# Issuing the seven Strassen products of an MLP chunk between the up products of the next chunk

## The chip, the cores and the metric

The kernel runs on one core of a Trainium2 chip. A core has five engines with instruction queues of their own: TensorE (PE; its weight loads appear as PEld), VectorE (DVE), ScalarE (ACT), GpSimd (POOL) and SyncE (SP), which here issues the DMAs. The metric is device time in microseconds, lower is better. A profile is of one execution.

## The reference

A two-layer encoder on 512 tokens of width 1024, in float32. What matters here is the MLP of a layer and what follows it:

```python
h = rmsnorm(x, g_ffn[i])
u = dwconv(h @ w_up[i], w_ffn_conv[i])       # 1024 -> 2 * 2816, then a width-3 convolution over tokens
a, val = u[..., :D_FF], u[..., D_FF:]
x = x + (jax.nn.silu(a) * val) @ w_down[i]   # 2816 -> 1024
h = rmsnorm(x, g_ple[i])
pg = jax.nn.sigmoid(h @ w_ple_gate[i])
x = x + pg * (p[i] @ w_ple[i])
```

## The kernel before

**Precision.** Every float32 matmul is three: both operands are split into a high part in float32r and a remainder (`wh`, `wl` of a weight; `hh`, `hl`, `ah`, `al`, `gh`, `gl` of activations), and `mm3` (lines 89 to 91) issues high by high, low by high, high by low. The split is a cast on ScalarE and a subtraction on VectorE (`weight` for loaded weights, lines 84 and 85; `split`, lines 94 and 95). The pool `wp` has five buffers each for `wh` and `wl`, used by all weights, and three for the raw loads.

**Up products.** The 2816 hidden columns are 22 tiles of 128. For tile `j`, `gated` computes two up products (gate and value), each 24 matmuls of 512 columns into a PSUM tile `ps_mm` or `ps_sc` (two buffers each). `taps` applies the convolution to a product (`fa`: one operation on ScalarE, line 619, two on VectorE, 620 and 621), SiLU goes over the gate, and their product is written to half of a tile `gv` (line 645).

**Down products.** A pair of tiles makes one `gv`. Two pairs (four tiles, eight up products) make a chunk whose down product is done by Strassen's scheme in the Winograd form. `combos` makes four sums of the activation blocks (`ss`) on POOL and splits all seven operands (`ah`, `al`). `seven` loads four blocks of `w_down` (`b11` to `b22`, one pool with `t3`, five buffers), makes four combinations of them on POOL (lines 553, 554, 556, 558), splits seven weights, and issues seven products of 12 matmuls each into PSUM accumulators `r1`, `r2`, `r3` (two tiles each, tags `tp`, three buffers, and `av`, one). After a product, `residual` adds its accumulator to `xs` on VectorE (line 599). Three of the products (P4, P6, P7) go on accumulating in `r1` after it has been read, and P5 in `r3`.

**Chunks.** 22 tiles are five chunks of four and one pair left over. In the kernel before, the leftover pair comes first, as an ordinary product (`proj` with two row blocks), and the five chunks follow. In the last chunk, `norm` of rows 0 and 1 is issued after the fifth product, of rows 2 and 3 after the seventh.

**Order.** The code is recorded by a framework that orders each engine's instructions by a list scheduler with a model of time; buffers of a pool are given out in that order. Inside `tc.manual_schedule` for TensorE, TensorE's instructions keep the order of the code; the other queues are still ordered by the scheduler. Before, the MLP has no such region.

Of the kernel before, what the change touches and what calls it, by code (L numbers as in the profile page):

```python
# [11 lines left out]
F32 = mybir.dt.float32  # L12
F32R = mybir.dt.float32r
# [22 lines left out]
FF = 2816  # L36
NJ = FF // P
EPS = 1e-6
CHUNKS = ((0, 2), (2, 6), (6, 10), (10, 14), (14, 18), (18, 22))
HS = S // 2  # L40
MAGIC = 12582912.0
LAG1 = 2
# [17 lines left out]
def encoder_kernel(ctx, tc, x_in, pT, pos, inv, w_a1, w_z, w_g, w_uq, w_ukv, w_au, w_cu, w_o,  # L60
# [15 lines left out]
    def psum(tag="mm"):  # L76
        return ps.tile([P, S], F32, tag=tag, name="ps_" + tag, bufs={"mm": 2, "av": 1, "sc": 2, "tp": 3}[tag])
# [15 lines left out]
    def split(hi, lo, src):  # L93
        nc.scalar.copy(hi, src)  # L94
        nc.vector.tensor_sub(lo, src, hi.bitcast(F32))  # L95
# [93 lines left out]
    def layer(l, first):  # L189
# [348 lines left out]
        def wsplit(raw):  # L538
            h = wp.tile([P, 1024], F32R, tag="wh", name="wh")
            lo = wp.tile([P, 1024], F32R, tag="wl", name="wl")  # L540
            split(h, lo, raw)
            return h, lo

        def seven(pool, ops, blocks, add, done, tags):
            b11, b12, b21, b22 = (pool.tile([P, 1024], F32, tag="rawd", name=n, bufs=5)
                                  for n in ("b11", "b12", "b21", "b22"))
            for i, b in ((2, b21), (0, b11), (1, b12), (3, b22)):
                nc.sync.dma_start(b, blocks[i])
            t3 = pool.tile([P, 1024], F32, tag="rawd", name="t3", bufs=5)
# [3 lines left out]
            g.tensor_tensor(t3, b22, b12, ALU.subtract)
            g.tensor_tensor(b12, b12, b11, ALU.subtract)
            wt1 = wsplit(b12)
            g.tensor_tensor(b11, b11, t3, ALU.add)
            wt2 = wsplit(b11)
            g.tensor_tensor(b21, b21, b11, ALU.subtract)

            def product(o, a, w, first):  # L560
                for tt in range(2):
                    tk = slice(tt * P, (tt + 1) * P)
                    for i, (h, lo) in enumerate(ops):
                        c = slice(i * 512, i * 512 + 512)
                        mm3(o[tt], (h[:, a, tk], lo[:, a, tk]), (w[0][:, c], w[1][:, c]),
                            first and i == 0, i == len(ops) - 1, not first)

            def out(o, rows, n):
                for tt in range(2):
                    add(2 * rows + tt, n, o[tt])  # L570

            r2 = [psum(tags[2]), psum(tags[3])]
            product(r2, 1, w21, True)
            out(r2, 0, 0)
            r1 = [psum(tags[0]), psum(tags[1])]
            product(r1, 0, w11, True)
            out(r1, 0, 0)
            r3 = [psum(tags[2]), psum(tags[3])]
            product(r3, 3, wt1, True)
            out(r3, 1, 1)  # L580
            product(r1, 4, wt2, False)
            out(r1, 0, 1)
            w22 = wsplit(b22)
            product(r3, 6, w22, False)
            out(r3, 0, 1)
            done(0)
            done(1)
            wt3 = wsplit(t3)
            product(r1, 5, wt3, False)
            out(r1, 1, 1)  # L590
            wt4 = wsplit(b21)
            product(r1, 2, wt4, False)
            out(r1, 1, 0)
            done(2)
            done(3)

        def residual(t, n, o):
            c = slice(n * 512, n * 512 + 512)
# [30 lines left out]
            for i in range(NE):  # L629
                ws(eo[i][:, c], ew[i], hT, KD, P, 0, c)  # L630
        g3 = load_gain(l, 2, ff)
        def gated(j, v):
            av = []
            for i in (2 * j, 2 * j + 1):
                if i < NE:
                    o = eo[i]
                else:
                    w = weight(w_up[l, i])
                    o = psum("sc" if i % 2 else "mm")
                    ws(o, w, hT, KD, P, 0)  # L640
# [4 lines left out]
            nc.vector.tensor_tensor(v[:, j % 2, :], av[0], av[1], ALU.mult)

        for c, (j0, j1) in enumerate(CHUNKS):
            ops = []
            for j in range(j0, j1, 2):
                v = ff.tile([P, 2, S], F32, tag="gv", name="gv", bufs=2)  # L650
                gated(j, v)
                gated(j + 1, v)
                if c:
                    ops.append(combos(ff, v))
                else:
                    gh, gl = (ff.tile([P, 2, S], F32R, tag="gt", name=n, bufs=8) for n in ("gh", "gl"))
                    split(gh, gl, v)
            last = j1 == NJ
            if c:
                seven(ff, ops, w_down[l, 4 * c - 2:4 * c + 2], residual,  # L660
                      (lambda t: norm(t, g3, ff)) if last else (lambda t: None),
                      ("mm", "mm", "sc", "sc") if last else ("tp", "tp", "tp", "av"))
            else:
                KTOT = 2
                proj((lambda k, q: gh[:, k, q], lambda k, q: gl[:, k, q]), range(2), w_down[l], residual, ("tp",))
# [8 lines left out]
        KTOT = 2  # L674
# [33 lines left out]
def _layout(i):  # L708
    f = {n: np.asarray(a) for n, a in i.items()}
    w_in = f["w_in"]  # L710
    o_cb, o_cc, o_cx, o_g = A1, A1 + CW, A1 + 2 * CW, A1 + 3 * CW

    def mtiles(w):
        l, k, n = w.shape
        return w.reshape(l, k // P, P, n // P, P).transpose(0, 3, 2, 1, 4)

    def interleave(*ws):
        return np.stack([mtiles(w) for w in ws], 2)

    def halves(w):  # L720
        l, k, n = w.shape
        return w.reshape(l, k // 256, 2, P, 2, 512).transpose(0, 4, 1, 3, 2, 5).reshape(l, k // 128, P, 1024)

    z = interleave(w_in[:, :, o_cc:o_cx], w_in[:, :, o_cx:o_g], w_in[:, :, o_cb:o_cc])
    g = interleave(w_in[:, :, o_g:o_g + D], w_in[:, :, o_g + D:])
    uq = f["w_uq"].reshape(L, QL, H, DQK)
    uq = np.concatenate([uq[..., :DN].reshape(L, QL, H * DN), uq[..., DN:].reshape(L, QL, H * DR)], -1)
    ukv = f["w_ukv"].reshape(L, KVL, H, 2, 64).transpose(0, 1, 3, 2, 4).reshape(L, KVL, 1024)

    def up2(w):  # L730
        l, k, n = w.shape
# [35 lines left out]
    return {n: np.ascontiguousarray(a) for n, a in res.items()}
# [18 lines left out]
```

## Time and profile before

| | |
|---|---|
| Median of three runs | 1600.34 us (1596.21, 1600.34, 1600.38) |
| Profiled execution | 1597.0 us, its span 1595.2 us |
| TensorE busy | 1547.1 us, 97% of the span |
| VectorE busy | 1040.9 us, 65% |
| ScalarE busy | 726.7 us, 46% |
| GpSimd busy | 286.9 us, 18% |
| Mean granted TensorE clock | 0.991 |

A line such as `L599` is a line of the kernel before. The matmuls of line 89 to 91 carry the names of their output tile and operands, by which the products are told apart: `ps_mm` or `ps_sc` from `hh` and `wh` is an up product, `ps_tp` or `ps_av` from `ah` a product of `seven`. Busy time of TensorE is that of overlapping matmuls; their starts tell the rate.

### The profile page before, as it was taken

To read this page: it belongs to the slowest core of one execution; us is meant where nothing else is said; L and a number is where in the kernel's file an instruction comes from. 1 tells how busy PE (TensorE), PEld (TensorE's weight loads), DVE (VectorE), ACT (ScalarE), POOL (GpSimd) and SP (SyncE) were. 2 spreads that over 40 slices of the span, in tenths; PEclk is the share of its full clock that TensorE was granted. 3 is DMA by queue.
4 is the path that set the end of the run, shared out by engine and by line. 5 is a ranking of instruction groups with operands and counts; after the bars stand their busy time and mean duration, and the time that the engine had idled before them with its cause. 6 is when DMAs were issued, how large, how long until landed. Compare 5 with 4: busy or idle time off the path is not lost.

```text
span 1595.2 us, 18618 instructions
## 1 busy us (share of the span) xinstructions
PE 1547.1 (97%) x7168; PEld 1263.9 (79%) x7168; DVE 1040.9 (65%) x1384; ACT 726.7 (46%) x1136; POOL 286.9 (18%) x273
## 2 busy tenths in 40 slices
PE   7999999999999989999999999999999989998998
PEld 6888888888877778787888888888887878787776
DVE  7787543346776776778477774433566776767673
ACT  5578723234333333335374886322344333333452
POOL 2700000001223132321045000000012142222300
PEclk9999999999999999999999999999999999999999
DMA  6211222315231322213242112222342322323031
GB/s 205 89 53 40 64 94 94 106 53 187 70 116 66 119 65 94 94 65 99 63 132 80 40 40 80 93 94 78 113 149 70 119 66 92 102 83 106 27 99 60
DMA packets 41433, 142.08 MB, mean 89 GB/s; under 512 B 5761, under 2 KB 6273, under 8 KB 41345
## 3 DMA queue, kind: packets, MB, share of 16 engines
q1 hardware_dynamic: 41344, 140.90, 26.8%
q8 instruction: 56, 0.92, 0.2%
q14 instruction: 33, 0.26, 0.1%
HBM read 138.78 MB, written 2.10 MB: 88 GB/s over the span
## 4 chain that ended last, share of the span: by engine, by line
PE 88%; DVE 5%; POOL 3%; ACT 2%; issue 1%; DMA 0%; DVEq 0%; POOLq 0%; ACTq 0%
PE ps_mm L90 14%; PE ps_mm L89 14%; PE ps_mm L91 14%; PE ps_sc L89 10%; PE ps_sc L90 10%; PE ps_sc L91 10%; PE ps_tp L89 3%; PE ps_tp L90 2%; PE ps_tp L91 2%; PE ps_tp L429 2%; PE ps_av L89 1%; PE ps_av L90 1%; PE ps_av L91 1%; PE ps_tp L126 1%; POOL rs L100 1%; PE ps_av L441 1%
## 5 line engine op out<-in xcount | busy, mean ns | idle before, releaser
L84 ACT CAST wh<-raw 128x1024 fp32r<-128x1024 f32 (+1 forms) x210 | 219.1, 1046 | 415.8 <-PE ps_mm L90 125.0
L85 DVE TENSOR_TENSOR wl<-raw,wh 128x1024 fp32r<-128x1024 f32 (+1 forms) x210 | 273.6, 1304 | 198.0 <-ACT wh L84 191.5
L89 PE MATMUL ps_mm<-hh,wh 128*128 128x512 f32 (+1 forms) x832 | 326.4, 392 | 0.4 <-DVE ycv L356 0.4
L90 PE MATMUL ps_mm<-hl,wh 128*128 128x512 f32 (+1 forms) x832 | 322.7, 388 | 0.0
L91 PE MATMUL ps_mm<-hh,wl 128*128 128x512 f32 (+1 forms) x832 | 322.4, 387 | 0.0
L91 PEld LDWEIGHTS ps_mm<-hh,wl 128*128 128x128 f32 x832 | 156.6, 188 | 34.8
L89 PEld LDWEIGHTS ps_mm<-hh,wh 128*128 128x128 f32 x832 | 156.7, 188 | 33.0 <-DVE ycv L356 0.9
L90 PEld LDWEIGHTS ps_mm<-hl,wh 128*128 128x128 f32 x832 | 156.9, 189 | 32.4 <-DVE hl L95 0.4
L90 PE MATMUL ps_sc<-hl,wh 128*128 128x512 f32 (+1 forms) x368 | 142.1, 386 | 0.0
L91 PE MATMUL ps_sc<-hh,wl 128*128 128x512 f32 (+1 forms) x368 | 142.1, 386 | 0.0
L89 PE MATMUL ps_sc<-hh,wh 128*128 128x512 f32 (+1 forms) x368 | 142.0, 386 | 0.0
L99 POOL TENSOR_SCALAR ms<-ms 128x1 f32<-128x1 f32 (+2 forms) x40 | 14.1, 353 | 694.1 <-ACT junk L118 669.0
L95 DVE TENSOR_TENSOR wl<-b,wh 128x1024 fp32r<-128x1024 f32 x60 | 82.5, 1375 | 74.9 <-ACT wh L94 74.9
L89 PE MATMUL ps_tp<-wh,ah 128*128 128x512 f32 x176 | 73.4, 417 | 26.3 <-ACT ah L94 17.6
L599 DVE TENSOR_TENSOR xs<-xs,ps_tp 128x512 f32<-128x512 f32 x104 | 69.9, 681 | 21.3 <-PE ps_tp L91 20.9
L94 ACT CAST wh<-b 128x1024 fp32r<-128x1024 f32 x60 | 62.8, 1047 | 44.1 <-PE ps_sc L90 22.1
L90 PEld LDWEIGHTS ps_sc<-hl,wh 128*128 128x128 f32 x368 | 69.3, 188 | 15.4
L89 PEld LDWEIGHTS ps_sc<-hh,wh 128*128 128x128 f32 x368 | 69.3, 188 | 15.3
L91 PEld LDWEIGHTS ps_sc<-hh,wl 128*128 128x128 f32 x368 | 69.3, 188 | 15.3
L90 PE MATMUL ps_tp<-wl,ah 128*128 128x512 f32 x176 | 72.3, 411 | 0.0
L643 ACT ACTIVATE fa<-fa 128x512 f32<-128x512 f32 x44 | 27.8, 631 | 94.7 <-DVE fa L621 94.7
L91 PE MATMUL ps_tp<-wh,al 128*128 128x512 f32 x176 | 70.1, 406 | 0.0
(271 smaller groups left out, 3081.3 us busy)
## 6 DMA issues: line engine op xcount, KB each, us to landing
raw<-in_w_up_dram SPq DMA_DIRECT2D x88, 512.0 KB, 3.4
b<-in_w_down_dram SPq DMA_DIRECT2D x40, 512.0 KB, 3.4
raw<-in_w_g_dram SPq DMA_DIRECT2D x32, 512.0 KB, 3.5
raw<-in_w_z_dram SPq DMA_DIRECT2D x24, 512.0 KB, 3.5
raw<-in_w_o_dram SPq DMA_DIRECT2D x16, 512.0 KB, 3.4
raw<-in_w_pg_dram SPq DMA_DIRECT2D x16, 512.0 KB, 3.5
raw<-in_w_au_dram SPq DMA_DIRECT2D x8, 512.0 KB, 3.4
raw<-in_w_cu_dram SPq DMA_DIRECT2D x8, 512.0 KB, 3.5
```

What stands on the lines that cost most here:

```text
L84: nc.scalar.copy(h, raw)
L85: nc.vector.tensor_sub(lo, raw, h.bitcast(F32))
L89: nc.tensor.matmul(o, st[0], mv[0], start=start, stop=False, skip_group_check=more)
L90: nc.tensor.matmul(o, st[0], mv[1], start=False, stop=False, skip_group_check=more)
L91: nc.tensor.matmul(o, st[1], mv[0], start=False, stop=stop, skip_group_check=more)
L94: nc.scalar.copy(hi, src)
L95: nc.vector.tensor_sub(lo, src, hi.bitcast(F32))
L100: nc.gpsimd.tensor_tensor(r, ms, negh[:, :n], ALU.pow)
L126: nc.tensor.transpose(tp[:, j * P:(j + 1) * P], ht[:, j * P:(j + 1) * P], ident)
L429: nc.tensor.transpose(tp[:, k * P:(k + 1) * P], pe[:, k * P:(k + 1) * P], ident)
L599: nc.vector.tensor_tensor(xs[:, t, c], xs[:, t, c], o, ALU.add)
L643: nc.scalar.activation(a, a, AF.Silu)
```

## The change

`seven` becomes a generator with a `yield` after its loads and first two weight splits and after each product but the last. A list `work` holds it, and `step` runs it on by one product. `gated` calls `step` after each up product, so that a chunk's products stand one by one behind the up products of the next chunk; the weight splits and POOL combinations inside `seven` are moved to one or two products before their use. The MLP stands in a manual region for TensorE. The five chunks come first, the leftover pair last, with its four up products taking one, two, two and no steps behind them, so that the last two products stand behind the fourth; then `proj` of the leftover rows, whose second half of columns calls `norm`. The rows of `w_down` are laid out in the new order on the host. Line numbers below `seven` shift: 599 is now 602, 619 to 621 are 622 to 624, 645 is 656, 556 and 558 are 572 and 578.

```diff
-CHUNKS = ((0, 2), (2, 6), (6, 10), (10, 14), (14, 18), (18, 22))
+NQ = NJ // 4
...
             w21 = wsplit(b21)
             w11 = wsplit(b11)
             g.tensor_tensor(t3, b22, b12, ALU.subtract)
             g.tensor_tensor(b12, b12, b11, ALU.subtract)
-            wt1 = wsplit(b12)
-            g.tensor_tensor(b11, b11, t3, ALU.add)
-            wt2 = wsplit(b11)
-            g.tensor_tensor(b21, b21, b11, ALU.subtract)
+            yield
...
-            r2 = [psum(tags[2]), psum(tags[3])]
+            r2 = [psum("tp"), psum("tp")]
             product(r2, 1, w21, True)
             out(r2, 0, 0)
-            r1 = [psum(tags[0]), psum(tags[1])]
+            g.tensor_tensor(b11, b11, t3, ALU.add)
+            wt1 = wsplit(b12)
+            yield
+            r1 = [psum("tp"), psum("av")]
             product(r1, 0, w11, True)
             out(r1, 0, 0)
-            r3 = [psum(tags[2]), psum(tags[3])]
+            g.tensor_tensor(b21, b21, b11, ALU.subtract)
+            wt2 = wsplit(b11)
+            yield
+            r3 = [psum("tp"), psum("tp")]
             product(r3, 3, wt1, True)
             out(r3, 1, 1)
+            w22 = wsplit(b22)
+            yield
             product(r1, 4, wt2, False)
             out(r1, 0, 1)
-            w22 = wsplit(b22)
+            wt3 = wsplit(t3)
+            yield
             product(r3, 6, w22, False)
             out(r3, 0, 1)
-            done(0)
-            done(1)
-            wt3 = wsplit(t3)
+            wt4 = wsplit(b21)
+            yield
             product(r1, 5, wt3, False)
             out(r1, 1, 1)
-            wt4 = wsplit(b21)
+            yield
             product(r1, 2, wt4, False)
             out(r1, 1, 0)
-            done(2)
-            done(3)
...
+        work = []
+        def step(n=1):
+            for _ in range(n):
+                if work and next(work[0], work) is work:
+                    work.pop(0)
+        def gated(j, v, steps=(1, 1)):
...
+                step(n)
...
+        region = tc.manual_schedule(engines={mybir.EngineType.PE})
+        region.__enter__()
+        for c in range(NQ):
+            ops = []
+            for j in range(4 * c, 4 * c + 4, 2):
+                v = ff.tile([P, 2, S], F32, tag="gv", name="gv", bufs=2)
+                gated(j, v)
+                gated(j + 1, v)
+                ops.append(combos(ff, v))
+            step(2)
+            work.append(seven(ops, w_down[l, 4 * c:4 * c + 4]))
+            step()
+        v = ff.tile([P, 2, S], F32, tag="gv", name="gv", bufs=2)
+        gated(4 * NQ, v, (1, 2))
+        gated(4 * NQ + 1, v, (2, 0))
+        gh, gl = (ff.tile([P, 2, S], F32R, tag="gt", name=n, bufs=8) for n in ("gh", "gl"))
+        split(gh, gl, v)
+        step(10)
+        region.__exit__(None, None, None)
```

Three places of the built program follow. Numbers behind names tell buffers apart; `[waits ...]` names the engine whose semaphore a row waits for.

TensorE at the end of a chunk before: the last three matmuls of up product U7 (`ps_sc`), then at once the first products of the chunk, with the operands of its first pair (`ah_3747`).

```order
L89 MATMUL ps_sc_3870<-hh_71,wh_3866 128x512
L90 MATMUL ps_sc_3870<-hl_72,wh_3866 128x512
L91 MATMUL ps_sc_3870<-hh_71,wl_3867 128x512
L89 MATMUL ps_tp_3942<-wh_3922,ah_3747 128x512 [waits Activation_49]
L90 MATMUL ps_tp_3942<-wl_3923,ah_3747 128x512
L91 MATMUL ps_tp_3942<-wh_3922,al_3748 128x512 [waits DVE_49]
```

After nine more matmuls comes the first that needs the pair computed last (`ah_3905`). TensorE now, at the end of U0 of the third chunk (`ps_mm_4177`), then P1 of the second.

```order
L90 MATMUL ps_mm_4177<-hl_72,wh_4173 128x512
L91 MATMUL ps_mm_4177<-hh_71,wl_4174 128x512
L89 MATMUL ps_tp_4207<-wh_4160,ah_3939 128x512
L90 MATMUL ps_tp_4207<-wl_4161,ah_3939 128x512
L91 MATMUL ps_tp_4207<-wh_4160,al_3940 128x512
L89 MATMUL ps_tp_4207<-wh_4160,ah_4143 128x512 [waits Activation_49]
L90 MATMUL ps_tp_4207<-wl_4161,ah_4143 128x512
L91 MATMUL ps_tp_4207<-wh_4160,al_4144 128x512 [waits DVE_49]
```

P1 moved behind the 24 matmuls of U0; its fourth and sixth matmul wait for the second pair.

SyncE before, loads of `w_up` tiles and of a chunk's four `w_down` blocks:

```order
L81 DMA raw_4592<-in_w_up_dram 128x1024 [waits DMAHW7_49,DMAHW2_49,DVE_49]
L548 DMA b21_4837<-in_w_down_dram 128x1024 [waits DVE_49,Pool_49]
L548 DMA b11_4835<-in_w_down_dram 128x1024 [waits DVE_49,Pool_49]
L548 DMA b12_4836<-in_w_down_dram 128x1024 [waits DVE_49]
L548 DMA b22_4838<-in_w_down_dram 128x1024 [waits DVE_49]
L81 DMA raw_4628<-in_w_up_dram 128x1024 [waits DMAHW0_49,DVE_49]
```

SyncE now:

```order
L548 DMA b21_4614<-in_w_down_dram 128x1024 [waits DMAHW6_49,DVE_49,Pool_49]
L81 DMA raw_4409<-in_w_up_dram 128x1024 [waits DMAHW3_49,DVE_49]
L548 DMA b11_4612<-in_w_down_dram 128x1024 [waits DMAHW0_49,DVE_49,Pool_49]
L81 DMA raw_4463<-in_w_up_dram 128x1024 [waits DMAHW4_49,DVE_49]
L548 DMA b12_4613<-in_w_down_dram 128x1024 [waits DVE_49]
L81 DMA raw_4513<-in_w_up_dram 128x1024 [waits DMAHW5_49,DVE_49]
L548 DMA b22_4615<-in_w_down_dram 128x1024 [waits DVE_49]
```

The four block loads moved apart, each ahead of the load of an up weight.

VectorE at the end of the MLP before: the taps of the last up product (`fa_5739`), the gate product `gv` and the split of the last pair for Strassen products.

```order
L95 TENSOR_TENSOR wl_5849<-b22_5760,wh_5848 128x1024 [waits DMAHW6_49,PE_49,Activation_49]
L620 SCALAR_TENSOR_TENSOR fa_5739<-ps_sc_5714,wfc_3296,fa_5739 128x511 [waits Activation_49]
L621 SCALAR_TENSOR_TENSOR fa_5739<-ps_sc_5714,wfc_3296,fa_5739 128x511 [waits DVE_49]
L645 TENSOR_TENSOR gv_5599<-fa_5703,fa_5739 128x512 [waits DVE_49]
L95 TENSOR_TENSOR al_5750<-gv_5599,ah_5749 128x512 [waits Activation_49]
```

VectorE now, from the last up product (`fa_5791`) to the split of the leftover pair (`gl`); `wl_6014`, `wl_6052` and `wl_6092` belong to weights of the stages behind the MLP, the `xs` rows are additions of P6 and P7.

```order
L85 TENSOR_TENSOR wl_6014<-raw_6011,wh_6013 128x1024 [waits DMAHW5_49,PE_49,Activation_49]
L602 TENSOR_TENSOR xs_70<-xs_70,ps_tp_5646 128x512 [waits PE_49]
L623 SCALAR_TENSOR_TENSOR fa_5791<-ps_sc_5766,wfc_3296,fa_5791 128x511 [waits Activation_49]
L602 TENSOR_TENSOR xs_70<-xs_70,ps_av_5647 128x512 [waits PE_49]
L624 SCALAR_TENSOR_TENSOR fa_5791<-ps_sc_5766,wfc_3296,fa_5791 128x511 [waits DVE_49]
L85 TENSOR_TENSOR wl_6052<-raw_6049,wh_6051 128x1024 [waits DMAHW6_49,Activation_49]
L602 TENSOR_TENSOR xs_70<-xs_70,ps_tp_5646 128x512 [waits PE_49]
L656 TENSOR_TENSOR gv_5553<-fa_5719,fa_5791 128x512 [waits DVE_49]
L602 TENSOR_TENSOR xs_70<-xs_70,ps_av_5647 128x512 [waits PE_49]
L85 TENSOR_TENSOR wl_6092<-raw_6089,wh_6091 128x1024 [waits DMAHW7_49,Activation_49]
L95 TENSOR_TENSOR gl_5797<-gv_5553,gh_5796 128x1024 [waits Activation_49]
```

The additions of two products and two more weight splits moved in between the last up product and the split of its pair.

More of the change, by code (lines that the diff above doesn't have):

```diff
@@ L542, in wsplit, with seven @@
             return h, lo
-        def seven(pool, ops, blocks, add, done, tags):
-            b11, b12, b21, b22 = (pool.tile([P, 1024], F32, tag="rawd", name=n, bufs=5)
+        def seven(ops, blocks):
+            b11, b12, b21, b22 = (ff.tile([P, 1024], F32, tag="rawd", name=n, bufs=5)
                                   for n in ("b11", "b12", "b21", "b22"))
@@ L548, in seven @@
                 nc.sync.dma_start(b, blocks[i])
-            t3 = pool.tile([P, 1024], F32, tag="rawd", name="t3", bufs=5)
+            t3 = ff.tile([P, 1024], F32, tag="rawd", name="t3", bufs=5)
             g = nc.gpsimd
@@ L569, in out @@
                 for tt in range(2):
-                    add(2 * rows + tt, n, o[tt])
-            r2 = [psum(tags[2]), psum(tags[3])]
+                    residual(2 * rows + tt, n, o[tt])
+            r2 = [psum("tp"), psum("tp")]
             product(r2, 1, w21, True)
             out(r2, 0, 0)
-            r1 = [psum(tags[0]), psum(tags[1])]
+            g.tensor_tensor(b11, b11, t3, ALU.add)
+            wt1 = wsplit(b12)
+            yield
+            r1 = [psum("tp"), psum("av")]
             product(r1, 0, w11, True)
             out(r1, 0, 0)
-            r3 = [psum(tags[2]), psum(tags[3])]
+            g.tensor_tensor(b21, b21, b11, ALU.subtract)
+            wt2 = wsplit(b11)
+            yield
+            r3 = [psum("tp"), psum("tp")]
             product(r3, 3, wt1, True)
             out(r3, 1, 1)
+            w22 = wsplit(b22)
+            yield
             product(r1, 4, wt2, False)
             out(r1, 0, 1)
-            w22 = wsplit(b22)
+            wt3 = wsplit(t3)
+            yield
             product(r3, 6, w22, False)
             out(r3, 0, 1)
-            done(0)
-            done(1)
-            wt3 = wsplit(t3)
+            wt4 = wsplit(b21)
+            yield
             product(r1, 5, wt3, False)
             out(r1, 1, 1)
-            wt4 = wsplit(b21)
+            yield
             product(r1, 2, wt4, False)
             out(r1, 1, 0)
-            done(2)
-            done(3)
         def residual(t, n, o):
@@ L631, in layer @@
         g3 = load_gain(l, 2, ff)
-        def gated(j, v):
+        work = []
[4 more added lines that the diff above has]
+        def gated(j, v, steps=(1, 1)):
             av = []
-            for i in (2 * j, 2 * j + 1):
+            for i, n in zip((2 * j, 2 * j + 1), steps):
                 if i < NE:
@@ L644, in gated @@
                 av.append(a)
+                step(n)
             nc.vector.tensor_tensor(v[:, j % 2, :], av[0], av[1], ALU.mult)
-        for c, (j0, j1) in enumerate(CHUNKS):
+        region = tc.manual_schedule(engines={mybir.EngineType.PE})
+        region.__enter__()
+        for c in range(NQ):
             ops = []
-            for j in range(j0, j1, 2):
+            for j in range(4 * c, 4 * c + 4, 2):
                 v = ff.tile([P, 2, S], F32, tag="gv", name="gv", bufs=2)
@@ L652, in layer, with after_d @@
                 gated(j + 1, v)
[L653 to L665, printed above, removed]
+                ops.append(combos(ff, v))
[9 more added lines that the diff above has]
+        region.__exit__(None, None, None)
+        def after_d(t, n, o):
+            residual(t, n, o)
+            if n == 1:
+                norm(t, g3, ff)
+        KTOT = 2
+        proj((lambda k, q: gh[:, k, q], lambda k, q: gl[:, k, q]), range(2), w_down[l, 4 * NQ:], after_d, ("mm", "sc"))
         ph = ff.tile([P, 2, S], F32R, tag="gt", name="ph", bufs=8)
@@ L755, in _layout @@
         "w_up": up.reshape(L, 2 * NJ, P, 1024),
-        "w_down": np.concatenate([halves(down[:, :256]), quads(down[:, 256:])], 1),
+        "w_down": np.concatenate([quads(down[:, :512 * NQ]), halves(down[:, 512 * NQ:])], 1),
         "w_pg": halves(f["w_ple_gate"]),
```

## The prediction, on record before the change was run

> **What bounds the kernel now.** I read the page's engine table first, then TensorE's waits, the windows over the MLP stage, and the timeline of one seam. The page, and all that TensorE waited for (line, releaser, us, times, longest):
>
> ```profile
> PE 1547.1 (97%) x7168; PEld 1263.9 (79%) x7168; DVE 1040.9 (65%) x1384; ACT 726.7 (46%) x1136; POOL 286.9 (18%) x273
> PE 88%; DVE 5%; POOL 3%; ACT 2%; issue 1%; DMA 0%; DVEq 0%; POOLq 0%; ACTq 0%
> ```
>
> ```profile
> PE ps_tp L89 <- ACT ah L94: 17.6, 8, 2.2
> PE ps_tp L126 <- DVE ht L123: 8.9, 2, 8.0
> PE ps_tp L89 <- DVE xs L599: 8.7, 7, 2.1
> PE ps_sc L89 <- DVE fa L621: 3.2, 2, 1.6
> ```
>
> TensorE is the bound. Its matmul work is the same after the change, so only its waits, and stretches at a lower clock, can be won. Three of these four rows lie in the MLP stage: the products of `seven` wait for their activations (`ah`) or for the additions to `xs`; two wait for `fa`.
>
> I call the eight up products of a chunk U0 to U7 and the seven Strassen products P1 to P7, in the order of their issue. The windows run from the first matmul of P1 to that of the next chunk's P1 (four in each layer), then from the last P1 of a layer until 42 of its matmuls have started. Columns: stretch, length, busy PE, PEld, DVE, ACT, POOL, granted clock, DMA share, GB/s.
>
> ```profile
> 361.00:439.90 78.90, 78.90 (x412) 66.72 (x411) 54.33 (x61) 32.12 (x43) 16.70 (x11) 1.00 0.39 130
> 439.90:509.21 69.31, 66.19 (x277) 52.43 (x276) 50.72 (x55) 26.61 (x34) 18.47 (x12) 0.98 0.28 92
> 509.21:578.52 69.31, 66.61 (x277) 52.90 (x276) 50.73 (x55) 26.65 (x34) 18.36 (x12) 0.98 0.28 91
> 578.52:649.38 70.86, 66.59 (x277) 52.89 (x276) 50.06 (x55) 26.53 (x34) 19.01 (x12) 0.98 0.28 90
> 649.38:718.70 69.32, 66.60 (x277) 52.90 (x276) 50.72 (x55) 26.64 (x34) 19.09 (x12) 0.98 0.23 76
> 1228.05:1295.39 67.34, 65.07 (x277) 51.75 (x276) 51.12 (x55) 26.66 (x34) 18.08 (x12) 1.00 0.29 95
> 1295.39:1366.26 70.87, 66.60 (x278) 52.90 (x276) 50.20 (x55) 26.54 (x34) 19.06 (x12) 0.98 0.28 89
> 1366.26:1435.55 69.29, 66.59 (x277) 52.89 (x276) 50.72 (x55) 26.64 (x34) 18.43 (x12) 0.98 0.28 92
> 1435.55:1506.40 70.85, 66.58 (x277) 52.89 (x276) 51.86 (x55) 26.54 (x34) 18.05 (x12) 0.98 0.22 75
> 718.70:732.04 13.34, 10.56 (x44) 7.56 (x42) 11.54 (x14) 7.49 (x9) 2.62 (x3) 1.00 0.13 41
> 1506.40:1520.53 14.13, 12.08 (x43) 8.77 (x42) 11.60 (x14) 7.59 (x9) 2.60 (x3) 0.88 0.12 37
> 515.00:518.00 3.00, 3.00 (x9) 2.33 (x8) 1.30 (x3) 1.05 (x1) 1.42 (x2) 0.50 0.00 0
> ```
>
> Before the first seam (361 to 439.9) TensorE has no gap. An undisturbed up product takes 5.63 us from its first matmul to the next product's (24 matmuls, 0.2346 us each):
>
> ```profile
> 481.10 0.40 PE L89 MATMUL ps_sc<-hh,wh 128*128 128x512 f32 x1
> ...
> 486.73 0.40 PE L89 MATMUL ps_mm<-hh,wh 128*128 128x512 f32 x1
> ```
>
> So a Strassen product (12 matmuls) takes 2.815, and a chunk without loss 8 x 5.63 + 7 x 2.815 = 64.75 us. The eight full stretches sum to 557.15; 8 x 64.75 is 518.0: **39.2 us lost at eight seams**. The two last stretches sum to 27.47 for 2 x 9.85: **7.8 us**.
>
> The timeline of the seam at 509 shows the loss (start, duration, line, work, the idle time before it):
>
> ```profile
> 508.98 0.39 PE L91 MATMUL ps_sc<-hh,wl 128*128 128x512 f32 x1
> 509.18 1.05 ACT L94 CAST wh<-b 128x1024 fp32r<-128x1024 f32 x1 [0.67 <-PE ps_sc L90]
> 509.21 0.40 PE L89 MATMUL ps_tp<-wh,ah 128*128 128x512 f32 x1
> 510.14 0.69 ACT L619 ACTIVATE fa<-ps_sc,wfc 128x512 f32<-128x512 f32 x1
> 510.26 1.23 DVE L95 TENSOR_TENSOR wl<-b,wh 128x1024 fp32r<-128x1024 f32 x1 [2.48 <-ACT wh L94]
> 511.40 0.74 DVE L620 SCALAR_TENSOR_TENSOR fa<-ps_sc,wfc,fa 128x511 f32<-128x511 f32 x1
> 512.97 0.69 DVE L645 TENSOR_TENSOR gv<-fa 128x512 f32<-128x512 f32 x1
> 513.70 0.92 ACT L94 CAST ah<-gv 128x512 fp32r<-128x512 f32 x2 [2.88 <-DVE gv L645]
> 514.35 1.56 DVE L95 TENSOR_TENSOR al<-gv,ah 128x512 fp32r<-128x512 f32 x2 [0.68 <-ACT ah L94]
> 514.37 0.50 PE L89 MATMUL ps_tp<-wh,ah 128*128 128x512 f32 x1 [2.20 <-ACT ah L94]
> 515.43 0.63 PE L90 MATMUL ps_av<-wl,ah 128*128 128x512 f32 x1
> 515.85 0.63 PE L89 MATMUL ps_tp<-wh,ah 128*128 128x512 f32 x1
> 517.61 1.23 DVE L95 TENSOR_TENSOR al<-ss,ah 128x1024 fp32r<-128x1024 f32 x1 [1.70 <-ACT ah L94]
> 519.49 0.50 PE L89 MATMUL ps_tp<-wh,ah 128*128 128x512 f32 x1 [0.50 <-DVE xs L599]
> ...
> 519.83 0.40 PE L90 MATMUL ps_tp<-wl,ah 128*128 128x512 f32 x1
> ```
>
> U7 ends, TensorE does the half of P1 and P2 that needs the first pair of columns, and then waits for taps, product, split: `ah` of the second pair comes 5 us after U7, `al` of the sums 9.6 us (517.61 + 1.23 - 509.21). After the wait the matmuls come 0.42 us apart and the window at 515 grants half the clock.
>
> **The change, part by part.** *P1 moves behind the next chunk's U0.* U0 covers 5.63 us. P1 needs the new `ah` at its fourth matmul, 5.63 + 3 x 0.2346 = 6.33 after U7, and `al` at its sixth, 6.80. The chain above, with the same operations in the same order in the built program, has the first `ah` part at about 5.1 (513.70 plus two thirds of 0.92) and the first `al` part at about 6.2 (514.35 plus two thirds of 1.56). No wait, with 0.6 us to spare. P3, the first to need the sums, starts 22.5 after U7 against 9.6. The seams cost 0: minus 39.2.
>
> *P2 to P7 between U1 and U7.* The five `wh`/`wl` buffers now alternate between ups and products. In the built order U2's split waits for P1's release, U3's for P2's, and so on: U plus P, 8.45 us, from release to use. The chain for U2: after U0 (5.63) a cast of 1.05 and a `wl` of 1.23, two additions to `xs` and one tap (0.68, 0.68, 0.74), `al` of the sums 1.23, then U2's own `wl` 1.23: 12.5 where 16.9 is the deadline. Cost 0, hidden by U1 and P2; without that cover it would be some 2.3 us per product. VectorE's work per chunk stays at about 50.7 us (55 operations), now in 64.75: 78%.
>
> *POOL and SP.* From the page, an up load's time to landing, and two of the four combinations of `w_down` blocks on POOL (busy us, mean ns, idle before):
>
> ```profile
> raw<-in_w_up_dram SPq DMA_DIRECT2D x88, 512.0 KB, 3.4
> ```
>
> ```profile
> L558 POOL TENSOR_TENSOR b<-b,b 128x1024 f32<-128x1024 f32 x4 | 13.1, 3268 | 0.3
> ...
> L556 POOL TENSOR_TENSOR b<-b,t 128x1024 f32<-128x1024 f32 x4 | 9.6, 2402 | 4.6 <-DVE wl L95 4.6
> ```
>
> The combinations now stand apart: the last two wait behind the split of P2's weight, near the end of the chunk before. That split follows P6 (at 50.6 of the chunk) by a cast and some five short VectorE operations, so about 54; with 2.40 and 3.27 POOL is done near 61 of 64.75, and P4's and P7's weights, which need the results, are split later. On SP the four block loads stand between up loads instead of in a row. The last, `b22`, waits for the split of P6's weight, some 25 us after U0's start (U2's end at 22.5, a cast, a `wl`); the up load queued behind it is U7's, cast after P5, at 42. At 3.4 us per load it is 10 us too early. Cost 0, hidden by the buffers filled a chunk ahead; if SP stood still for those 10 us as well, U7 would wait.
>
> *The leftover rows come last.* The first chunk's leftover product (48 matmuls) moves to the end; it waited for nothing where it was and carries over at the same length. At the end P6 and P7 (5.63 us) alone cover the chain from the last up product to `gh`. In the built order VectorE does `wl` of the next weights first (start 1.05 after, as above, 1.23), then addition, tap, addition, tap, another `wl`, addition, gate: 1.05 + 1.23 + 0.68 + 0.74 + 0.68 + 0.74 + 1.23 + 0.68 + 0.69 = 7.7; ScalarE's cast of 1024 columns 1.05 more: 8.8. TensorE waits 3.2 us, and I add 0.1 for the two halves of P7, which follow P6 directly and wait for its additions. Half clock behind such a wait: 9 matmuls (the x9 of the window at 515) x (0.42 - 0.2346) = 1.7. Together 5.0 per layer, where the old tails lost 7.8 in all: plus 10.0 minus 7.8. Bounds per layer: 0 (the rows' starts overlap a little, as 510.26 and 511.40 do, and the split comes in time) and 8 (the four norms, of which two came before the last products, now all stand behind the last rows and come late too). I take 5.0, the sum of the rows.
>
> **Sum**, against the profiled execution's own 1597.0 (span 1595.2): 1597.0 - 39.2 - 7.8 + 10.0 = **1560.0**. The median of the runs shown is 3.3 higher, and they differ by 4.2 among themselves; I keep 1560.
>
> **Rivals.** *P1 still waits.* Its margin is 0.6 us and `wl` stands ahead of the chain. A big POOL operation stretched `wl` by 1.0:
>
> ```profile
> 455.97 2.82 POOL L553 TENSOR_TENSOR t<-b,b 128x1024 f32<-128x1024 f32 x1 [8.78 <-DMA b<-in_w_down_dram]
> ```
>
> ```profile
> 457.64 2.23 DVE L85 TENSOR_TENSOR wl<-raw,wh 128x1024 fp32r<-128x1024 f32 x1
> ```
>
> If the last combination slides into the seam, ten first products wait about 0.5 us: 1565. If each also brings the half clock (1.7): 1582. Against it: that combination ends some 3 us before U7 by the count above, and the 0.50-us wait at 519.49 was followed by a matmul at the full rate.
>
> *The tails' waits keep the full clock.* The old tail at 718.70 waited too and its window shows 1.00, as does the seam at 1228; the tail at 1506 shows 0.88 and seven seams 0.98. With full clock, 1.7 us less per layer: 1556.6. [...] Beyond this, tails without any cost would give 1550.
>
> *Slower: late weights.* VectorE falls behind, and each of U2 to U7 in eight chunks (48 places) waits for its `wl`. The point of decision is the 8.45 us from release to use: rows give about 4, and if POOL stretches two splits and the sums' `al` by 1.0 each, 7. At 10 us each place loses 1.5: 1560 + 72 = 1632. [...]
>
> *Nothing won*: the wait only moves, from P1 to a later product on the same chain, and TensorE loses the same: 1597. The 22.5 against 9.6 us of P3 speaks against it.
>
> **Chances.** Forecast 0.58, full clock in the tails 0.20, P1 waits 0.12, slower 0.06, nothing won 0.04. The range reaches from tails without cost to P1 with half clock, 1550 to 1582, and leaves out the last two and the far ends. Faster by over 0.3% (about 4.8 us, what a measurement of this kernel can tell) 0.90, same 0.04, slower 0.06.
>
> **What would show it.** Right: stretches from P1 to P1 of 64.8 us at clock 1.00; no wait of `ps_tp` for `ah` but in the tail; one wait of `ps_mm` for `gh` of about 3 us per layer. Wrong: `ps_mm` or `ps_sc` of the ups waiting for `wl` (slower rival), or `ps_tp` for `al` with a granted clock below 1 (P1 waits).

## The result, and the profile after

The changed kernel takes **1555.23 us** (median of four runs, 1554.85 to 1555.39) against 1599.07 us for the kernel before on the same chip: ratio 0.9728, 95% interval 0.9711 to 0.9745. The forecast was 1560, in a range of 1550 to 1582. The profiled execution took 1555.39 us (span 1553.6) against 1597.0: 41.6 us less. The engines' row of the page:

```profile
PE 1531.8 (99%) x7168; PEld 1257.4 (81%) x7168; DVE 1017.7 (66%) x1384; ACT 727.9 (47%) x1136; POOL 293.8 (19%) x273
```

All that TensorE waited for (line, releaser, us, times, longest), down to 0.8 us:

```profile
PE ps_tp L126 <- DVE ht L123: 8.6, 3, 7.5
PE ps_mm L89 <- ACT gh L94: 4.5, 2, 2.3
PE ps_mm L90 <- DVE wl L85: 1.3, 3, 0.9
PE ps_tp L126 <- DVE hl L95: 0.8, 1, 0.8
```

The rows for `ah` (17.6 us) and `xs` (8.7 us) are gone. In the MLP only the wait for `gh` is left, once per layer. The windows from P1 to P1 in the first layer, then the two tails, from the end of the last up product until 34 matmuls have started (columns as in the prediction):

```profile
411.90:476.37 64.47, 64.47 (x278) 51.87 (x276) 47.80 (x56) 26.66 (x33) 18.59 (x13) 1.00 0.29 98
476.37:540.84 64.47, 64.47 (x278) 51.89 (x277) 47.81 (x56) 26.65 (x33) 18.59 (x13) 1.00 0.30 98
540.84:605.30 64.46, 64.46 (x277) 51.89 (x276) 47.81 (x56) 26.66 (x33) 18.59 (x13) 1.00 0.30 99
605.30:669.77 64.47, 64.47 (x278) 51.90 (x276) 47.82 (x56) 26.65 (x33) 18.60 (x13) 1.00 0.28 90
700.59:712.74 12.15, 9.89 (x36) 7.34 (x34) 10.07 (x12) 5.68 (x6) 0.00 (x0) 0.86 0.42 131
1469.15:1479.84 10.69, 8.43 (x36) 6.23 (x34) 9.64 (x12) 5.70 (x6) 0.00 (x0) 1.00 0.38 114
```

A chunk takes 64.47 us with TensorE busy throughout at full clock; 276 matmuls make 0.2336 us each. Against this the eight full stretches of before (557.15 in sum) had lost 41.4. The tails lose 12.15 + 10.69 - 68 x 0.2336 = 7.0, the old ones 27.47 - 84 x 0.2336 = 7.8. In all 41.4 + 7.8 - 7.0 = 42.2 for the measured 41.6.

One seam after (timeline; U7 ends at 535.2, U0 runs to 540.8, then P1):

```profile
536.26 1.23 DVE L85 TENSOR_TENSOR wl<-raw,wh 128x1024 fp32r<-128x1024 f32 x1 [3.49 <-ACT wh L84]
538.97 0.69 DVE L656 TENSOR_TENSOR gv<-fa 128x512 f32<-128x512 f32 x1
539.70 0.93 ACT L94 CAST ah<-gv 128x512 fp32r<-128x512 f32 x2 [2.88 <-DVE gv L656]
540.35 1.58 DVE L95 TENSOR_TENSOR al<-gv,ah 128x512 fp32r<-128x512 f32 x2 [0.69 <-ACT ah L94]
541.53 0.39 PE L89 MATMUL ps_tp<-wh,ah 128*128 128x512 f32 x1
541.99 0.40 PE L91 MATMUL ps_tp<-wh,al 128*128 128x512 f32 x1
541.94 1.67 DVE L95 TENSOR_TENSOR wl<-b,wh 128x1024 fp32r<-128x1024 f32 x1
```

The chain is as late as it was; TensorE is no longer there to wait. The first `ah` part (two thirds of 0.93) is ready at 540.3 and needed at 541.53, the first `al` part at 541.4 and needed at 541.99: about 0.6 us to spare.

The tail of the first layer, and the first row behind the wait in the second:

```profile
701.63 1.23 DVE L85 TENSOR_TENSOR wl<-raw,wh 128x1024 fp32r<-128x1024 f32 x1 [4.00 <-ACT wh L84]
705.29 1.21 DVE L85 TENSOR_TENSOR wl<-raw,wh 128x1024 fp32r<-128x1024 f32 x1
707.02 0.68 DVE L656 TENSOR_TENSOR gv<-fa 128x512 f32<-128x512 f32 x1
707.74 1.05 ACT L94 CAST gh<-gv 128x1024 fp32r<-128x1024 f32 x1
708.83 0.79 PE L89 MATMUL ps_mm<-wh,gh 128*128 128x512 f32 x1 [2.26 <-ACT gh L94]
709.42 0.63 PE L90 MATMUL ps_mm<-wl,gh 128*128 128x512 f32 x1
```

```profile
1477.40 0.50 PE L89 MATMUL ps_mm<-wh,gh 128*128 128x512 f32 x1 [2.26 <-ACT gh L94]
1477.74 0.40 PE L90 MATMUL ps_mm<-wl,gh 128*128 128x512 f32 x1
```

The same wait of 2.26 us is followed by half clock (0.427 us per matmul) in the first layer and by none in the second.

### The profile page after: what moved, and what is told of

Same layout as the page of the kernel before. It is cut to its first block, busy times and chain, and to the rows that moved or that the text cites. A ratio compares the mean times of both kernels' runs of the same rounds, so it can differ in the third digit from the quotient of the medians.

```text
span 1553.6 us, 18593 instructions
## 1 busy us (share of the span) xinstructions
PE 1531.8 (99%) x7168; PEld 1257.4 (81%) x7168; DVE 1017.7 (66%) x1384; ACT 727.9 (47%) x1136; POOL 293.8 (19%) x273
## 4 chain that ended last, share of the span: by engine, by line
PE 88%; issue 4%; POOL 3%; DVE 2%; ACT 1%; DMA 1%; SPq 0%; POOLq 0%; DVEq 0%; ACTq 0%
PE ps_mm L90 14%; PE ps_mm L89 13%; PE ps_mm L91 13%; PE ps_sc L90 10%; PE ps_sc L89 10%; PE ps_sc L91 10%; PE ps_tp L90 3%; PE ps_tp L91 3%; PE ps_tp L89 3%; PE ps_tp L429 2%; PE ps_av L89 2%; PE ps_av L91 1%; PE ps_av L90 1%; POOL rs L100 1%; PE ps_av L441 1%
## 5 line engine op out<-in xcount | busy, mean ns | idle before, releaser
L85 DVE TENSOR_TENSOR wl<-raw,wh 128x1024 fp32r<-128x1024 f32 (+1 forms) x210 | 263.9, 1260 | 205.4 <-ACT wh L84 194.5
L95 DVE TENSOR_TENSOR wl<-b,wh 128x1024 fp32r<-128x1024 f32 x60 | 78.7, 1312 | 47.7 <-ACT wh L94 47.6
L90 PE MATMUL ps_tp<-wl,ah 128*128 128x512 f32 x200 | 79.2, 396 | 0.0
L89 PE MATMUL ps_tp<-wh,ah 128*128 128x512 f32 x200 | 79.1, 395 | 0.0
L91 PE MATMUL ps_tp<-wh,al 128*128 128x512 f32 x200 | 79.1, 395 | 0.0
```

The lines of the kernel that those rows point to most:

```text
L85: nc.vector.tensor_sub(lo, raw, h.bitcast(F32))
L89: nc.tensor.matmul(o, st[0], mv[0], start=start, stop=False, skip_group_check=more)
L90: nc.tensor.matmul(o, st[0], mv[1], start=False, stop=False, skip_group_check=more)
L91: nc.tensor.matmul(o, st[1], mv[0], start=False, stop=stop, skip_group_check=more)
```

## The experiments

The theory: the gain is TensorE's seams, because a product stands one up product behind its activations. Rivals: it is the move of the leftover pair, the pinned order, or just the spreading. Each kernel is the changed kernel with one edit. They ran on several chips, on which the kernel before took 1598.66 to 1600.37 us; differences of 2 us or less between two rows are not read as differences.

| Kernel | Median (range), us | Ratio to before, 95% |
|---|---|---|
| block at the seam | 1630.04 (1629.62 to 1630.58) | 1.0190, 1.0175 to 1.0205 |
| P1 alone at the seam | 1624.58 (1623.93 to 1625.23) | 1.0156, 1.0141 to 1.0171 |
| block behind U0 | 1590.80 (1589.11 to 1593.12) | 0.9950, 0.9933 to 0.9966 |
| leftover pair first | 1556.49 (1556.32 to 1558.00) | 0.9742, 0.9726 to 0.9758 |
| order not pinned | 1555.69 (1553.03 to 1557.03) | 0.9731, 0.9716 to 0.9745 |
| tail covered by four products | **1549.37** (1548.85 to 1549.48) | 0.9685, 0.9671 to 0.9700 |
| tail without cover | 1566.02 (1565.61 to 1566.91) | 0.9796, 0.9780 to 0.9813 |
| two more VectorE operations | 1596.46 (1594.77 to 1601.12) | 0.9995, 0.9982 to 1.0008 |
| the same, P1 behind U1 | 1555.18 (1553.78 to 1556.75) | 0.9730, 0.9713 to 0.9746 |
| four weight buffers | 1581.04 (1579.17 to 1583.68) | 0.9892, 0.9877 to 0.9908 |
| four buffers, no combinations | 1555.82 (1554.47 to 1556.30) | 0.9732, 0.9716 to 0.9748 |

### Where the products stand

The whole block at its own seam:

```diff
-            step()
+            step(9 if c < NQ - 1 else 1)
```

> At the eight inner seams the seven products are issued in one block right behind U7 of their own chunk; the leftover pair stays last, the last chunk's products stay spread over it, and TensorE's order stays pinned. If the gain lies in covering the seam: P1's fourth matmul waits for the new `ah`, 4.4 us (5.1 after U7 less the 0.7 of its first three), the additions cost what they cost before (8.7 us in 7 places, 1.1 per seam), half clock 1.7: 7.2 per seam, 8 x 7.2 = 58 above 1555, so 1613; at least the old loss of about 5 per seam, 1596. If the gain came from the pinned order, from the leftover pair or from the run's clock as such: within 5 us of 1555.

P1 alone at the seam:

```diff
-            step()
+            step(2)
...
-        gated(4 * NQ, v, (1, 2))
+        gated(4 * NQ, v, (0, 2))
```

> Only P1 moves: it stands right behind U7 of its own chunk, P2 to P7 behind U0 to U5 of the next; the two products in the tail stay two. Cover theory: one product at the seam waits as long as seven do, 4.4 us for `ah`, 0.4 more for `al`, half clock 1.7: 6.5 per seam, here at 10 seams with the last chunk's: 65, so 1620, or 1603 without half clock. P2 and after wait for nothing. Rival, that the gain is shared out over the spread products: one of seven gives back a seventh of the 42 us, 1561.

The whole block behind U0:

```diff
-                gated(j, v)
+                gated(j, v, (7, 1) if c and j == 4 * c else (1, 1))
```

> All seven products stand in one block behind U0 of the next chunk (8 seams; the tail is unchanged). Cover theory: U0's 5.6 us hide the activations, since P3 starts 11.2 us after U7 where `al` of the sums is ready at 9.6. What is left is the block itself: additions to `xs` in the accumulators used again, 1.1 per seam as before, and weight splits at 2.3 us per product of 2.8, about 1: 2 per seam, 1555 + 16 = 1571. VectorE has 14 additions, six splits, two taps and the sums' `al` in the block, some 20 us for 19.7; if it falls behind, 5 per seam, 1595. Rival, that one covering product is all that counts: 1555.

The waits of TensorE that these edits brought, in that order:

```profile
PE ps_tp L89 <- ACT ah L94: 34.3, 8, 4.3
PE ps_tp L89 <- DVE xs L602: 14.7, 8, 2.0
```

```profile
PE ps_tp L89 <- ACT ah L94: 43.4, 10, 4.4
```

```profile
PE ps_tp L89 <- DVE xs L602: 25.2, 15, 2.7
```

The block at the seam costs 75 us over the changed kernel, 9.4 per seam. That is more than the kernel before lost: there the scheduler ran the halves of P1 and P2 that were ready first and waited 2.2 us for `ah`; the written order waits 4.3, as expected. Waits make 49.0 of the 75, and 14 stretches at half clock (114 matmuls at 0.19 us more each, against 8 in the changed kernel) about 20; the rest, some 5, is not traced. The expectation fell short in two terms: it had one such stretch per seam, and 8.8 us for the additions, which made TensorE wait 14.7. P1 alone at the seam costs nearly as much: 69 us at ten seams, 43.4 of it waits and about 22 half clock (121 matmuls). So not a share of the gain sits in each product: one product too early loses all of it.

The block behind U0 has no wait for `ah` or `al` and still costs 35.6. My 16 were too few; the larger figure in the text, 5 per seam (1595), is nearer. It is the accumulators that wait, in the row for `xs` (15 times, 25.2 us). In the timeline of one block, splits of up weights stand between VectorE's additions; two of them take 2.94 and 2.21 us instead of 1.21 while POOL makes combinations of `w_down` blocks (491.80 to 494.21 and 494.29 to 497.54). The last row is a matmul that waited for an addition:

```profile
492.35 2.94 DVE L85 TENSOR_TENSOR wl<-raw,wh 128x1024 fp32r<-128x1024 f32 x1
495.21 0.68 DVE L602 TENSOR_TENSOR xs<-xs,ps_tp 128x512 f32<-128x512 f32 x1
495.81 0.67 DVE L602 TENSOR_TENSOR xs<-xs,ps_av 128x512 f32<-128x512 f32 x1
496.41 2.21 DVE L85 TENSOR_TENSOR wl<-raw,wh 128x1024 fp32r<-128x1024 f32 x1
...
501.69 0.47 PE L89 MATMUL ps_tp<-wh,ah 128*128 128x512 f32 x1 [2.63 <-DVE xs L602]
```

So the place of the products acts in two ways. Of the 75 us between the block at the seam and the changed kernel, U0's cover is worth 39 and the spreading another 36. These are not shares of the 44 us won over the kernel before, which orders the halves of P1 and P2 in another way than either block. The prediction had counted both as one term.

### The move of the leftover pair, and the pinned order

Leftover pair first, the last chunk's products uncovered at the end (the rows of `w_down` and the norms as before):

```diff
+        gated(0, v)
+        gated(1, v)
+        split(gh, gl, v)
         for c in range(NQ):
...
+                if j == 2:
+                    proj(..., w_down[l], residual, ("tp",))
...
         region.__exit__(None, None, None)
+        step(10)
```

> The interleaving is kept for four chunks, the leftover pair comes first as before (its product behind the fourth up product of the first chunk), and the last chunk's seven products stand at the end, without an up product to cover them, in the order and with the buffers that the kernel before gives them. It undoes the move of the leftover pair alone. Two old tails cost 13.34 - 9.81 = 3.5 and 14.13 - 9.81 = 4.3; the changed kernel's two tails cost 4.2 and 2.8 in its profile. So 1555.2 + 7.8 - 7.0 = 1556: the move by itself is worth nothing that can be measured, and all of the gain is the eight seams'. Rival, that the leftover pair as a cover for the last chunk's products is worth a seam per layer (5 each): 1565.

The order not pinned:

```diff
-        region = tc.manual_schedule(engines={mybir.EngineType.PE})
-        region.__enter__()
```

> The interleaved code without the pinned region: the scheduler orders TensorE's instructions. In the built order P1 to P7 stay behind U0 to U6 (P1 and P2 both inside U1's neighbourhood, their halves that need the first pair ahead), and behind the leftover rows' first `gh` matmuls stands a product of `w_ple`. If the place of the products is what wins, not the pinning: 1555, within 4 us either way, no wait for `ah`. If the pinned order itself matters: waits at the seams of 2 us or more, 1570 to 1597.

Both agree with the changed kernel within their intervals, and neither waits over 0.4 us for `ah`. The move by itself is worth nothing that can be measured, and nor is the pinning once the code stands in this order.

### The tail

Four products behind the last up product instead of two:

```diff
-        gated(4 * NQ, v, (1, 2))
-        gated(4 * NQ + 1, v, (2, 0))
+        gated(4 * NQ, v, (1, 1))
+        gated(4 * NQ + 1, v, (1, 0))
```

> The leftover pair's four up products take one, one, one and no steps instead of one, two, two and none, so that four products (P4 to P7, 11.2 us) stand behind the last up product instead of two. The chain to `gh` took 8.2 us, so its wait (2.3 per layer, some 0.4 around it) and the half clock of one layer (1.5) go: 1555.2 - 6.9 = 1548; P4 to P7 in a row wait for additions, some 0.2 each: 1549. Rival, that the norms behind the leftover rows are what is late, so that the wait only moves: 1555.

5.9 us less than the changed kernel, and the best of all. In the window from 1130 us to the end, which has the second layer's MLP, TensorE's one listed wait is now:

```profile
PE ps_sc L89 <- ACT hh L94: 0.4, 1, 0.4
```

No wait for `gh` is left in either layer; it did not move to the norms. None behind the last up product:

```diff
-        gated(4 * NQ, v, (1, 2))
-        gated(4 * NQ + 1, v, (2, 0))
+        gated(4 * NQ, v, (2, 2))
+        gated(4 * NQ + 1, v, (3, 0))
```

> The leftover pair's four up products take two, two, three and no steps, so that no product stands behind the last up product; all else is as in the changed kernel. Tail theory: the chain to `gh` is 8.2 us from the last up product, and the two products of 5.6 that covered it are gone: the wait grows from 2.3 to 7.9 per layer, 2 x 5.6 = 11.2. P5, P6 and P7 in a row behind the third up product add some 1 us per layer for additions. Half clock in both layers, not in one: 1.5 more. 1555.2 + 11.2 + 2 + 1.5 = 1570. If half clock lasts in proportion to the wait (2.26 us were followed by about 1.5 lost), 5 per layer: 1577. Rival, that the norms behind the rows set the tail's end and the wait for `gh` only lies beside them: 1555 to 1560.

10.8 more than the changed kernel: below the 1570 expected, well above the rival's 1560. Half clock lasted 6.8 us in each layer (26 matmuls in all, against 8), more than the expected one stretch, but the wait is not 7.9 per layer:

```profile
PE ps_mm L89 <- ACT gh L94: 10.8, 2, 5.4
PE ps_tp L89 <- DVE xs L602: 1.8, 2, 0.9
```

```profile
708.26 1.23 DVE L85 TENSOR_TENSOR wl<-raw,wh 128x1024 fp32r<-128x1024 f32 x1 [4.15 <-ACT wh L84]
...
710.96 0.69 DVE L656 TENSOR_TENSOR gv<-fa 128x512 f32<-128x512 f32 x1
```

The chain from the last up product to the first matmul with `gh` shrank from 8.2 us to 5.6 (707.2 to 712.79): without products behind it, VectorE has only the two taps between the first `wl` and `gv`, and no addition or second `wl`. Two covering products cover 5.6 us but make the chain 2.7 longer.

### The margin of P1

Two operations of 0.69 us each ahead of the second pair's split:

```diff
+                if j % 4:
+                    nc.vector.tensor_scalar_mul(v, v, 1.0)
+                    nc.vector.tensor_scalar_mul(v, v, 1.0)
                 ops.append(combos(ff, v))
```

> Two more VectorE operations (the product `gv`, 1024 columns, times one, in place) ahead of the split of the second pair of every chunk, nothing else. The profile after shows the margin of P1 in one seam: `al` ready at 6.2 after U7 where P1's sixth matmul stands at 6.8, and `ah` at 5.1 where its fourth stands at 6.3. If the two operations take 1.2 us together, P1 waits 0.6 for `al` at ten seams, 1561; at 1.2 each, 1.8 per seam, 1573. Half clock behind such short waits: none (half clock, 1.7 each: 1590). Rival, that P1's cover is far wider than counted: 1555.

All of the gain is lost, 41 us for an expected 6 to 18 (35 with half clock at every seam). The two operations add 1.4 us to the chain, but P1's sixth matmul, due at 481.5 in the seam below, comes 3.0 us late where 0.8 (1.4 less the margin) would follow:

```profile
PE ps_tp L89 <- ACT ah L94: 13.6, 10, 1.4
PE ps_tp L91 <- DVE al L95: 12.2, 10, 1.2
```

```profile
479.89 0.69 DVE L668 TENSOR_SCALAR gv<-gv 128x1024 f32<-128x1024 f32 x1
480.32 1.05 ACT L94 CAST wh<-b 128x1024 fp32r<-128x1024 f32 x1 [4.04 <-PE ps_mm L90]
481.41 1.76 DVE L95 TENSOR_TENSOR wl<-b,wh 128x1024 fp32r<-128x1024 f32 x1 [0.82 <-ACT wh L94]
481.86 0.91 ACT L94 CAST ah<-gv 128x512 fp32r<-128x512 f32 x2
483.09 0.74 DVE L623 SCALAR_TENSOR_TENSOR fa<-ps_mm,wfc,fa 128x511 f32<-128x511 f32 x1
483.75 1.55 DVE L95 TENSOR_TENSOR al<-gv,ah 128x512 fp32r<-128x512 f32 x2
484.48 0.50 PE L91 MATMUL ps_tp<-wh,al 128*128 128x512 f32 x1 [1.23 <-DVE al L95]
```

U0 ends at 480.3, and the chain's second added operation at 480.6. The built order now differs from the changed kernel's on two engines. On ScalarE the cast of the next product's weight (1.05) and U0's first tap operation (0.68) stand ahead of the cast of `ah`, and on VectorE that weight's `wl` (1.76) and U0's next tap operation (0.74) ahead of `al`; in the seam of the changed kernel above, this `wl` stands behind `al`. The waits of both kinds make 25.8 of the 41, and eight stretches at half clock instead of one about 10. So the loss came as a step: the extra 1.4 us also cost the chain its place in two queues. Only this one length was run; from which length on the order changes is not shown. That P1's place is the cause shows when the products move one up product back and the operations stay:

```diff
-                gated(j, v)
+                gated(j, v, (1, 1) if j % 4 else (0, 1))
...
-        gated(4 * NQ, v, (1, 2))
-        gated(4 * NQ + 1, v, (2, 0))
+        gated(4 * NQ, v, (0, 2))
+        gated(4 * NQ + 1, v, (3, 0))
```

> As the run with two more VectorE operations ahead of the split (1596.5), but P1 to P7 stand behind U1 to U7 of the next chunk instead of U0 to U6; the tail still has two products. If those two operations cost time only because P1 stands one up product behind its activations, the cover grows from 5.6 to 11.2 us and all 41 us come back: 1555 to 1557. Rival, that VectorE's added 1.4 us per chunk, or what it pushes back behind it, is the cost wherever P1 stands: 1575 to 1596.

All 41 us come back; VectorE's added work costs nothing where it is covered.

### The slower rival, brought about

```diff
-    wp = ctx.enter_context(tc.tile_pool(name="wp", bufs=5))
+    wp = ctx.enter_context(tc.tile_pool(name="wp", bufs=4))
```

> Four buffers of `wh` and of `wl` instead of five, in the whole kernel. The weights of U1 to U7 then take the buffer that the up product before has released, and the cover from release to use falls from U plus P, 8.45 us, to P alone, 2.8. The split takes 2.3 (cast 1.05, `wl` 1.23), its `wl` is needed 0.5 after the start, so any VectorE operation of over 1 us ahead of it makes TensorE wait: about 1 us at each of 56 places in the chunks, 1555 + 56 = 1611, with waits of `ps_mm` and `ps_sc` for `wl`. This is the slower rival of the prediction brought about on purpose. Rival, that VectorE is free whenever a split comes: 1555; other stages that share the pool may add a few us.

```profile
PE ps_sc L91 <- DVE wl L85: 14.2, 8, 1.8
```

25.8 us lost, not 56: one wait per chunk instead of seven. The waits are 14.2 of it, and eight stretches at half clock instead of one (63 matmuls against 8) about 10. With 2.8 us of cover a split of 2.3 comes in time at six places, and at U5 it does not, since POOL works beside it (four rows of that place):

```profile
513.75 2.57 POOL L554 TENSOR_TENSOR b<-b,b 128x1024 f32<-128x1024 f32 x1
516.27 1.72 POOL L530 TENSOR_TENSOR ss<-ss,gv 128x256 f32<-128x256 f32 x1
513.99 3.41 DVE L85 TENSOR_TENSOR wl<-raw,wh 128x1024 fp32r<-128x1024 f32 x1
517.45 0.50 PE L91 MATMUL ps_sc<-hh,wl 128*128 128x512 f32 x1 [1.77 <-DVE wl L85]
```

To tell the buffers from POOL, the combinations go and the four buffers stay. This kernel leaves out a part of Strassen's scheme, so what it computes is not the down product; only its time is of use:

```diff
-            t3 = ff.tile([P, 1024], F32, tag="rawd", name="t3", bufs=5)
+            t3 = b22
...
-            g.tensor_tensor(t3, b22, b12, ALU.subtract)
-            g.tensor_tensor(b12, b12, b11, ALU.subtract)
```

(and the two behind P1 and P2)

> Four buffers of `wh` and `wl`, as in the run of 1581.0, and the four combinations of the `w_down` blocks on POOL are left out (the products take the blocks as loaded). In the run with four buffers each chunk waits once, 1.8 us for U5's `wl`, which took 3.4 us instead of 1.23 while POOL was making a combination. If POOL's work beside VectorE's is what makes that split late: no such wait, 1555. If the cover of one product (2.8 us) is too short by itself: the eight waits stay, 1575 to 1581.

The eight waits for `wl` are gone. The cover of one product is enough without POOL's combinations, and too little with them.

## Why the prediction was right, point by point

- **Seams cost nothing.** Right: the first layer's four stretches are 64.46 to 64.47 us at clock 1.00, against the promised 64.8. Their loss before was 41.4, not 39.2: the pitch is 0.2336 us, and I had worked with 0.2346, read from one up product; over eight chunks of 276 matmuls that makes 2.2.
- **P1's margin of 0.6.** Right to the tenth, and the two edits around it show that it carries the whole gain.
- **Weights need no wait, cover 8.45 us.** Right. With less cover the rival came true, but at 26 us and by POOL's hand.
- **POOL and SP cost nothing.** Right: the last combination ended 3.8 us before U7 did, where about 3 was counted, and no up product waited for a load. VectorE's work per chunk was not 50.7 but 47.8: about half of the difference is that the operations which run longer than usual add 3.2 us in a chunk, against 4.7 in the one from 509 us before; the rest is that more of its rows overlap.
- **Tails: plus 10.0.** The term that was mis-sized: 7.0. `gh` came 8.2 us after the last up product, not 8.8, because the chain's rows overlap; the wait is 2.4 from matmul to matmul, not 3.2; and half clock came in one layer, 8 matmuls or 1.5 us, not 9 in both. The edit with four products prices the whole tail at 5.9.
- **The move of the leftover rows.** I had priced old and new tails at 7.8 against 10.0; the run with the pair first says they are alike.
- **Rival "tails keep the full clock"**, 1556.6 with a chance of 0.20, came halfway true: one tail did. That the measured time lies nearer to 1556.6 than to 1560 is in part luck: 2.2 of the difference are the pitch, which has nothing to do with the tails. "P1 waits" and "late weights" were both one small edit away, and the first was priced too low: 1565 to 1582 stood in the prediction, and the edit that brought it about took 1596, beyond the range's end.

Together: 1560 less 2.2 for the pitch and 3.0 for the tails is 1554.8, for the 1555.4 of the profiled execution.

## What to carry over

Put a consumer one full piece of independent work behind its producer on the engine that bounds, and read the cover against the chain in one seam: here 5.6 us cover a chain of 5 to 6. Spread the pieces as well: in the block behind U0 the accumulations in a row waited 25.2 us for the additions between them. A small margin can be a cliff, since a later chain can also lose its place in the producing engines' queues: here 1.4 us more on the chain cost 41 us, and one more up product of cover gave it all back.

## What the runs showed of the hardware

**The half clock came on a grid of 3.41 us.** In the profiles of the kernel before and of the changed one, every recorded change of the granted clock (17 and 3) lies within 0.01 us of a grid of 3.4133 us, with a phase of its own in each; all nine stretches at half clock ahead of the last microseconds are one step of it long (8 before, 1 after). The two tails of the changed kernel, each with the step in which most of the wait for `gh` falls and the one behind it (columns as in the prediction; the second number is TensorE's busy time, the third from the end the granted clock):

```profile
705.28:708.69 3.41, 1.30 (x6) 0.72 (x4) 3.41 (x6) 2.00 (x3) 0.00 (x0) 1.00 0.46 144
708.69:712.10 3.41, 3.27 (x8) 2.59 (x9) 3.02 (x3) 1.04 (x2) 0.00 (x0) 0.50 0.62 192
1473.28:1476.69 3.41, 1.86 (x8) 1.15 (x7) 3.41 (x5) 1.43 (x2) 0.00 (x0) 1.00 0.42 130
1476.69:1480.10 3.41, 2.70 (x12) 2.20 (x13) 3.41 (x4) 1.61 (x2) 0.00 (x0) 1.00 0.61 199
```

In the first layer TensorE was idle for 2.11 us of one step, and the next ran at half clock; in the second the same wait was cut by the grid into 1.55 and 0.71, and the clock stayed full. The tails of this one execution differ by 1.46 us (12.15 and 10.69), about what the 8 matmuls at 0.427 us instead of 0.2336 make (1.5). From 400 us to the end of the two profiles, all nine steps at full clock with 1.86 to 2.20 us idle were followed by half clock, and none of the six with 1.37 to 1.66. That the idle time within a step decides, and so where a wait falls on the grid, is my reading of these 15 cases; no run moved a wait against the grid. It may also be why the kernel before, with waits of 0.5 to 2.2 us at every seam, spreads over 4.2 us and the changed one over 0.5. No run tested that, but the ten executions of the kernel with two more VectorE operations fit it: they go from 1594.8 us at a mean granted clock of 0.992 to 1601.1 at 0.988, and 0.004 of 1597 is 6.4 us.

**Some VectorE and POOL operations took longer beside each other.** In the run with four buffers a `wl` of an up weight, 1.23 us in the median of 30, took 3.41 beside two POOL operations, and POOL's `ss` beside it 1.72 against 1.09 in the changed kernel. Without the combinations the longest such `wl` between 440 and 700 us took 1.67. Not every pair does so: in the changed kernel a `gv` (from 507.42) took 2.90 us beside a combination of 3.34, against 0.69 in the seam shown above, and the `wl` that began 0.14 us before the same combination took 1.22.
